# Early first weights, an early third x and modulation products beside the last queries in a two-layer diffusion backbone

## The chip, the cores and the metric

The kernel runs on one core of a Trainium2 chip. The metric is the device time of one execution in microseconds (us). The core has five engines that work from queues of their own, in the order of these queues: PE (matrix products and transposes; the load of its stationary operand is shown as PEld), DVE, ACT and POOL (elementwise work), and SP, which only issues DMAs. POOL issues DMAs too. An engine that waits holds up all that stands behind in its queue.

## The reference

The reference is a backbone of two layers over 512 latent tokens x and 256 context tokens ctx, width 1024, all in fp32. Each layer has three sub-layers: a SwiGLU (hidden width 2816), a token mixer, and a second SwiGLU. Each of them is modulated by a vector c and sandwiched between two norms:

```
for l in range(2):
    mod = silu(c) @ w_ada[l] + b_ada[l]        # nine vectors of 1024; ctx has its own from c_ctx
    for each of the three sub-layers:
        u = rmsnorm(x) * g_pre * (1 + scale) + shift
        y = swiglu(u)  or  mixer(u)
        x = x + gate * rmsnorm(y) * g_post     # the SwiGLUs with another factor of 0.5
```

The even mixer (layer 0) projects u to two inputs of a gated linear recurrence (xa, ga) and to q, k, v of a windowed attention with rotary positions and a sink; the results of both go through one output projection. The odd mixer (layer 1) is a dense attention with normed q and k over context and latent tokens. Context tokens run through all of layer 0 and the first SwiGLU of layer 1; behind it they are needed only for keys and values.

## The kernel before

**Tokens and sub-layers.** The tokens are six tiles of 128 (t = 0, 1 context, 2 to 5 latent), in two chunks c of three tiles (384 columns); the last two sub-layers have four latent tiles, two per chunk. The loop in `body` (L1536 on) runs s = 0 to 5: SwiGLU, even mixer, SwiGLU, SwiGLU, odd mixer, SwiGLU.

**Products.** An fp32 operand is split into two fp32r halves by `halves` (L201): ACT copies it, rounded, into hi, DVE subtracts that from the operand into lo. Each product is then three matmuls (`mm3`, L208). Weights come as 128x1024 fp32 tiles into one of three buffers with the tag raw, and `weights` (L184) splits them, 512 columns at a time, into a hi and a lo buffer (tags whi and wlo, four each). `wtiles` with `one` takes tags ohi and olo instead, two each. `strassen` (L771) does gate and up of a SwiGLU with Strassen's scheme, `down` (L648) its second half, `type2` (L893) the projections of a mixer that leave tokens on partitions (q, k, v, and the output), `type1` (L938) those that leave channels there (xa, ga).

**The boundary between two sub-layers** (`boundary`, L503) runs for each tile of tokens when its y is complete in PSUM: a square with its sum on ACT (L513) and a product with the gate on DVE (L514) for either half, the sum, a reciprocal root (DVE L218, the power on POOL L220), a load of the tile's x by POOL's queue (L522) into one of two buffers with the tag bx, x + gate times normed y on DVE (L524), the store of x by POOL's queue (L528), and the next sub-layer's norm, ACT L426 and POOL L430. `make_u` (L388) then transposes on PE (L435), modulates on ACT and DVE (L409) and splits; where Strassen follows, `Sums` makes differences of blocks on DVE and POOL (L459 to L462). The tiles of chunk 0 are run later, as parts between products that still go on (`later`, `parts`); those of chunk 1 (here b_3, b_4, b_5 by their t) run at once, at the end of the sub-layer, when the products that remain are those of the next.

**Modulation vectors** are made beside other work. `ada_steps` (L113) is a generator for one group p of two 1024-wide vectors: eight steps k, each with two loads of 512 KB by SP's queue into raw tiles wa and four products of 32 columns (recorded as eight matmuls) into one PSUM bank. `tick` (L101) runs the next step of those that are queued in `bg`; groups 3 to 6 are queued at the even mixer (s = 1), 7 and 8 at the odd one (s = 4). `attention` ticks three times per group of heads (L1253), `ffn` once per block. For p > 2 the tiles wa lie in whi and wlo; while a group is under way its bank is held.

**Queries.** In the even mixer `qkv` (called per token tile as its sums are complete) applies the rotary position, splits q into halves qp and transposes them on PE (L1139) into a bank of the two with the tag ps, from which ACT copies (L1140). In the odd mixer `qf` does the same with oqT (L1437).

**What sets the order.** The program order isn't the order in the queues. A planner schedules the program with costs of its own and writes each engine's queue from that; a buffer of a tag is handed on in program order, so a tile waits for the buffer's last reader. `late` and `chain` pin single instructions. Any change of tag or of place in the program can so move work in all queues.

The change touches `weights`, `boundary`, `ada_steps`, `down`, `type1`, `type2`, the two query functions and the loop in `body`.

Of the kernel before, what the change touches and what calls it, by code (L numbers as in the profile page):

```python
# [17 lines left out]
P = 128  # L18
D = 1024
# [9 lines left out]
class Net:  # L29
# [32 lines left out]
    def consts(self):  # L62
        nc, cp, a = self.nc, self.cp, self.a
        self.ident = cp.tile([P, P], F32, name="ident")
        nc.gpsimd.dma_start(self.ident, a["ident"])
        self.sc = cp.tile([P, KD, 32], F32, name="sc")
        nc.sync.dma_start(self.sc, a["cvec"])
        nc.scalar.activation(self.sc, self.sc, AF.Silu)
        self.mhalf = cp.tile([P, 8], F32, name="mhalf")
        nc.vector.memset(self.mhalf, -0.5)  # L70
        self.gpre = cp.tile([P, 6, KD], F32, name="gpre")
        nc.gpsimd.dma_start(self.gpre, a["gpre"])
        self.identr = cp.tile([P, P], F32R, name="identr")
        nc.vector.tensor_copy(self.identr, self.ident)
        self.modc, self.gscale, self.growd = {}, {}, {}
        self.adatile = self.ps

    def c3(self, shape, dt, name):
# [34 lines left out]
    def ada_steps(self, p):  # L113
        nc, cp = self.nc, self.cp
        acc = self.adatile(f"ada{p}")
        for k in range(KD):
            raws = []
            for b in range(2):
                l, j = divmod(2 * p + b, 9)
                src, name = self.a["w_ada"][l, k * P:(k + 1) * P, j * D:(j + 1) * D], f"wa{p}_{k}{b}"  # L120
                if p > 2:

                    t = self.ws.tile([P, D], F32, tag=("whi", "wlo")[b], bufs=4, name=name)
                else:
                    t = self.ws.tile([P, D], F32, tag="bx", bufs=2, name=name)
                nc.sync.dma_start(t, src)
                raws += [t[:, 0:512], t[:, 512:]]
            for g in range(4):
                ins = nc.tensor.matmul(acc[32 * g:32 * g + 32, :], lhsT=self.sc[:, k, :],  # L129
                                       rhs=raws[g], start=(k == 0), stop=(k == KD - 1), skip_group_check=True)  # L130
                if p == 1:
                    self.late(ins)
            yield
# [47 lines left out]
        self.nc.sync.dma_start(t, src)  # L181
        return t

    def weights(self, src, name):  # L184

        raw, n = self.raw(src, name), src.shape[-1]
        hl = [[t[:, i:min(i + 512, n)] for t in ts] for ts in [self.wtiles(n, name)] for i in range(0, n, 512)]
        for i, (hi, lo) in enumerate(hl):
            self.halves(hi, lo, raw[:, i * 512:min(i * 512 + 512, n)])
        return hl  # L190

    def wtiles(self, n, name, one=False):

# [306 lines left out]
                ks = slice(2 * q, 2 * q + 2)  # L500
                self.net.halves(self.u[1][0][:, ks], self.u[1][1][:, ks], self.t4[q], late=True)

    def boundary(self, t, g, xsrc, xdst, nxt, name):  # L503


        nc, bp = self.nc, self.bp
# [1 line left out]
        y1 = bp.tile([P, D], F32, tag="by", bufs=3, name=name + "y")  # L508
        cut = [slice(0, 512), slice(512, D)]
        ss = bp.tile([P, 2], F32, tag="ss", bufs=6, name=name + "s")  # L510

        def half(i, y):
            nc.scalar.activation(self.junk(f"{name}{i}")[:, cut[i]], y, AF.Square, accum_out=ss[:, i:i + 1])  # L513
# [2 lines left out]
        def end():  # L516
# [1 line left out]
            r = self.rms_r(ss[:, 0:1], D, name + "p")  # L518

            def rest():  # L520
                x = bp.tile([P, D], F32, tag="bx", bufs=2, name=name + "x")
                nc.gpsimd.dma_start(x, xsrc(t))  # L522
                for c in cut if nxt is None else [slice(0, D)]:
                    nc.vector.scalar_tensor_tensor(x[:, c], y1[:, c], r[:, 0:1], x[:, c], op0=ALU.mult, op1=ALU.add)  # L524
                    if nxt is None:
                        nc.sync.dma_start(xdst(t)[:, c], x[:, c])
                if nxt is not None:
                    nc.gpsimd.dma_start(xdst(t), x)  # L528
                    self.normed(x, y1, name + "u")
# [118 lines left out]
    def down(self, l, s, n, hd, wt, g, start, finish, hook):  # L648
# [48 lines left out]
        def run():  # L697
# [4 lines left out]
            for k, (i, p) in enumerate(steps):  # L702

                a = min(k + self.AHEAD, len(steps) - 1, (i + 1) * np_ + 1 if p > np_ - 4 else len(steps))
                while todo and steps[a] not in ready:
                    make()
                if (i, p) in parts:
                    j, f = parts[i, p]
                    self.later[j][f]()
# [183 lines left out]
    def type2(self, nm, nk, lhs, nt, wsrc, finish, n=D, hook=None):  # L893
# [9 lines left out]
        for k in range(nk):  # L903
# [7 lines left out]
            if k < nk - self.STAG:  # L911
                for j in range(nt):
                    self.t2mm(accs[j], e, j, nk, n)
            else:
                last.append(e)
        for j in range(nt):

            for half in [0, 512] if nt == 4 and j == 3 else [None]:
# [19 lines left out]
    def type1(self, nm, src, nf, u, finish):  # L938

        for f0 in range(0, nf, 3):  # L940
            fs = range(f0, min(f0 + 3, nf))
            w = [self.weights(src(f), f"{nm}w{f}") for f in fs]
            self.rest()
            acc = [self.acc(f"{nm}a{f}") for f in fs]
            for c in range(2):
# [35 lines left out]
    def even(self, u, gate_i, finish):  # L981
# [132 lines left out]
        def qkv(t, acc):  # L1114
# [18 lines left out]
            nc.vector.tensor_sub(vt[:, :, 1, :], v3, vt[:, :, 0, :].bitcast(F32))  # L1133
            vs[t] = vt
            qt = qst["q"][:, t % 3]
            for h in range(2):
                tp = self.ps(f"qT{t}{h}").bitcast(F32R)
                for e in range(4):
# [231 lines left out]
    def odd(self, u, gate_i, finish):  # L1370
# [49 lines left out]
        def qf(t, acc):  # L1420
# [8 lines left out]
            for s in range(2):  # L1429
                i = 2 * (t - 2) + s  # L1430
                if i % 3 == 0:
                    qtt.append(sb.tile([P, 3, 8, P], F32R, tag=("u0h", "u0l", "u1h")[i // 3], name=f"oqt{i}"))
                qt.append(qtt[i // 3][:, i % 3])
            for h in range(2):
                tp = self.ps(f"oqT{t}{h}")
                for e in range(4):
# [100 lines left out]
    def body(self):  # L1537
# [9 lines left out]
        for s in range(6):  # L1547
            l, sub = divmod(s, 3)
            self.bg += [self.ada_steps(p) for p in need[s]]
            gate = (9 * l + 3 * sub + 2, s < 4)  # L1550
            if s == 5 or s == self.stop:
                un, sn = None, None
                dst = (lambda t: self.out[t * P:(t + 1) * P, :]) if self.stop < 5 else (lambda t: self.out[(t - 2) * P:(t - 1) * P, :])
# [7 lines left out]
            def start(c, j, g, s=s, un=un, sn=sn, xsrc=xsrc, dst=dst):  # L1561
                t = tl[s][c][j]
                nxt = None
                if un is not None:
                    c2, j2 = next((c2, m.index(t)) for c2, m in enumerate(tl[s + 1]) if t in m) if s != 3 else divmod(t, 3)
                    nxt = (9 * ((s + 1) // 3) + 3 * ((s + 1) % 3), un, c2, j2, sn)
                return self.boundary(t, g, xsrc, dst, nxt, f"b{s}_{t}")

            def finish(c, j, end, s=s, un=un, sn=sn):
                if c == 1 and un is not None and len(un) < 2:  # L1570
# [101 lines left out]
```

## Time and profile before

| what | us |
|---|---|
| median of three runs | 2600.66 |
| the three runs | 2595.28, 2600.66, 2603.51 |
| the profiled execution | 2593.1 |
| its span in the profile | 2591.3 |

The profile is of one execution. Times in it are us from the start of the span. The names b_3 to b_5 are the boundary tiles of t = 3 to 5, with the sub-layer's number left out; five boundaries (after s = 0 to 4) begin near 555, 904, 1438, 1948 and 2214 us. The last queries of the even mixer lie at 722 to 737 us, its attention at 737 to 840; those of the odd one at 2050 to 2075 and 2075 to 2165. In names of weights, w0110 is layer 0, second SwiGLU (the digit 1), block 1, gate (0; 1 is up); xaw0 is the first weight of xa, okv0w0 that of the odd mixer's keys and values, eo0w and oo0w those of the output projections.

### The profile page before, as it was taken

How to read it: one execution, taken by the hardware profiler on the slowest of the kernel's cores; microseconds unless marked ns; L12 is line 12 of the kernel's file. 1: busy time of each engine (PE TensorE's matmuls, PEld its weight loads, DVE VectorE, ACT ScalarE, POOL GpSimd, SP SyncE). 2: the span in 40 equal slices, each digit the busy share in tenths (PEclk: the TensorE clock that was granted, in tenths of full speed). 3: DMA queues.
4: the chain of work that ended last, by engine and by line, in shares of the span. 5: the costliest groups of instructions: out<-in, count | busy, mean ns of one | idle time of the engine just before them, and what ended most of it. 6: DMA issues, size and time to landing. Idle time of an engine off the chain costs nothing.

```text
span 2591.3 us, 36846 instructions
## 1 busy us (share of the span) xinstructions
PE 2489.6 (96%) x13683; PEld 2188.9 (84%) x13683; DVE 1877.6 (72%) x2946; ACT 1290.7 (50%) x2346; POOL 373.3 (14%) x472
## 2 busy tenths in 40 slices
PE   7999999998999989999999899999998899999998
PEld 5999997878855779999887899998876667899986
DVE  5877777577677687878757787887586666888843
ACT  4433335556665564443456544444465556655532
POOL 4000000122022130000002300001122221300000
PEclk8999999999999999999999999999999999999999
DMA  7677767651387435555776355558764652544552
GB/s 279 215 244 242 242 222 268 227 188 51 111 297 266 166 106 184 199 180 193 270 245 228 136 187 181 194 193 280 238 233 145 209 180 74 191 130 136 158 174 92
DMA packets 187588, 502.37 MB, mean 194 GB/s; under 512 B 17944, under 2 KB 51912, under 8 KB 187408
## 3 DMA queue, kind: packets, MB, share of 16 engines
q1 hardware_dynamic: 157520, 392.27, 44.6%
q0 software_dynamic: 29888, 107.74, 11.7%
q8 instruction: 107, 1.75, 0.3%
q14 instruction: 73, 0.60, 0.1%
HBM read 397.33 MB, written 102.61 MB: 193 GB/s over the span
## 4 chain that ended last, share of the span: by engine, by line
PE 78%; DVE 7%; issue 7%; DMA 3%; ACT 3%; POOL 2%; SPq 0%; POOLq 0%; DVEq 0%; ACTq 0%
PE px L784 18%; PE py L784 12%; PE pz L784 12%; PE dy L729 8%; PE dx L729 5%; PE d11a L935 5%; PE ada L129 3%; PE oq1a L935 1%; PE gu L211 1%; PE gu L212 1%; PE eo0a L935 1%; PE gu L210 1%; PE qkv1a L935 1%; DMA dw<-in_w_down_dram 1%; PE pT L1332 1%
## 5 line engine op out<-in xcount | busy, mean ns | idle before, releaser
L831 ACT ACTIVATE cp<-px 128x384 f32<-128x384 f32 (+1 forms) x160 | 73.2, 457 | 207.3 <-PE px L784 207.2
L837 ACT ACTIVATE h<-cp 128x768 f32<-128x768 f32 (+1 forms) x80 | 63.3, 792 | 195.7 <-DVE cp L861 138.8
L623 POOL DMA_DIRECT2D wt<-wt x33 | 17.7, 537 | 706.6 <-DVE wt L622 681.4
L129 PE MATMUL ada<-wa,sc 128*32 128x512 f32 x512 | 83.4, 610 | 0.5 <-DVE cols L144 0.4
L831 ACT ACTIVATE cp<-pz 128x384 f32<-128x384 f32 (+1 forms) x80 | 37.0, 463 | 87.2 <-PE pz L784 87.0
L861 DVE TENSOR_TENSOR cp<-px,cp 128x768 f32<-128x768 f32 (+1 forms) x80 | 70.8, 884 | 5.1 <-PE px L784 5.0
L839 DVE TENSOR_TENSOR h<-cp,h 128x768 f32<-128x768 f32 (+1 forms) x80 | 71.2, 891 | 2.2
L670 DVE TENSOR_TENSOR dh_2l<-dh,dh_2h 128x768 fp32r<-128x768 f32 x21 | 20.0, 953 | 70.3 <-ACT dh_2h L669 60.8
L220 POOL TENSOR_TENSOR b_2pr<-b_2pv,mhalf 128x1 f32<-128x1 f32 x6 | 9.6, 1602 | 355.7 <-DVE b_2pv L218 355.7
L811 DVE TENSOR_TENSOR w<-w,w 128x512 f32<-128x512 f32 x80 | 55.4, 692 | 2.7
L812 DVE TENSOR_TENSOR w<-w,w 128x512 f32<-128x512 f32 x80 | 55.4, 692 | 2.7
L810 DVE TENSOR_TENSOR w<-w 128x512 f32<-128x512 f32 x80 | 55.2, 691 | 2.4
L809 DVE TENSOR_TENSOR w<-w,w 128x512 f32<-128x512 f32 x80 | 54.6, 682 | 0.0
L613 POOL DMA_DIRECT2D wt<-in_w_down_dram x66 | 35.5, 537 | 113.1 <-DMA wt<-wt 113.1
L1324 POOL TENSOR_SCALAR p<-p,sm 128x256 f32<-128x256 f32 (+2 forms) x48 | 31.9, 677 | 136.3 <-DVE sm L1321 63.1
L846 DVE TENSOR_TENSOR cp<-py,cp 128x384 f32<-128x384 f32 (+1 forms) x80 | 41.4, 518 | 4.8 <-ACT cp L831 3.9
L670 DVE TENSOR_TENSOR dw_0slo<-dw,dw_0shi 128x1024 fp32r<-128x1024 f32 x21 | 25.7, 1225 | 25.6 <-ACT dw_0shi L669 25.3
L831 ACT ACTIVATE cp<-py 128x384 f32<-128x384 f32 (+1 forms) x80 | 36.3, 454 | 14.3 <-PE py L784 13.9
L1223 ACT ACTIVATE optb<-opT 128x512 fp32r<-128x512 f32 x48 | 28.6, 597 | 28.3 <-PE opT L1520 27.9
L1511 POOL TENSOR_SCALAR op<-op,osm 128x768 f32<-128x768 f32 x32 | 30.6, 956 | 75.8 <-DVE osm L1510 53.4
L854 DVE TENSOR_TENSOR cp<-pz,cp 128x384 f32<-128x384 f32 (+1 forms) x80 | 41.4, 518 | 0.0
L1223 ACT ACTIVATE ptb<-pT 128x512 fp32r<-128x512 f32 x44 | 26.3, 597 | 30.3 <-PE pT L1332 29.9
(5878 smaller groups left out, 9634.2 us busy)
## 6 DMA issues: line engine op xcount, KB each, us to landing
w<-in_wgu_dram SPq DMA_DIRECT2D x175, 512.0 KB, 3.5
wa<-in_w_ada_dram SPq DMA_DIRECT2D x138, 512.0 KB, 5.8
dh<-hd SPq DMA_DIRECT2D x105, 384.0 KB, 5.8
wt<-in_w_down_dram POOLq DMA_DIRECT2D x66, 512.0 KB, 4.6
wt<-wt POOLq DMA_DIRECT2D x66, 512.0 KB, 3.4
dw<-wt SPq DMA_DIRECT2D x60, 512.0 KB, 5.4
hd<-h SPq DMA_DIRECT2D x66, 384.0 KB, 2.8
dw<-in_w_down_dram SPq DMA_DIRECT2D x45, 512.0 KB, 7.0
```

What stands on the lines that cost most here:

```text
L129: ins = nc.tensor.matmul(acc[32 * g:32 * g + 32, :], lhsT=self.sc[:, k, :], rhs=raws[g], start=(k == 0), stop=(k == KD - 1), skip_group_ch ...
L729: nc.tensor.matmul(out, lhsT=x[xi][:, js], rhs=w[wi], start=first and p == 0 and xi == wi, stop=p == np_ - 1 and xi == 1, skip_group_check ...
L784: mm = lambda x, y, **kw: nc.tensor.matmul(out, lhsT=x, rhs=y, skip_group_check=True, **kw)
L810: chain(nc.vector.tensor_add(x1, x1, x2))
L811: chain(nc.vector.tensor_add(x2, x3, x2))
L812: chain(nc.vector.tensor_sub(x4, x4, x2))
L831: chain(nc.scalar.activation(t, src, AF.Copy))
L837: chain(nc.scalar.activation(hc, cp[f], AF.Silu))
L839: chain(nc.vector.tensor_mul(hc, cp[f], hc))
L861: chain(nc.vector.tensor_add(cp[1], x.unsqueeze(1).to_broadcast([P, 2, n]), cp[1]))
L935: mm(acc[:, h:min(h + 512, n)], lhsT=x[xi][:, js], rhs=w[h // 512][wi], start=(k == 0 and xi == 0 and wi == 0), stop=(k == nk - 1 and xi = ...
L1223: self.nc.scalar.activation(b[:, n, 0], tp, AF.Copy)
```

## The change

`ahead` is new. It loads the first weight tile of the next sub-layer (`coming`: xaw0, w0100, w1000, okv0w0, w1100 for s = 0 to 4) into raw and splits it into 512-wide tiles of the tags ohi and olo; `weights` later takes what lies in `pre` instead of loading. It's called in `down` at step (6, 8) of its products and in `type2` of the output projections before their last steps. `boundary` has a new argument: for the tiles of chunk 1 the load of x stands at the boundary's start, and that of t = 5 goes to the tag G1 (one buffer) instead of bx. In `ada_steps` groups 3 and 7 take raw tiles (even k) or G0 and G1 (odd k) rather than whi and wlo, and `qkv` and `qf` tick three steps at t = 4 and five at t = 5, ahead of the transposes. `type1` splits its weights of 1024 columns in one operation per engine rather than two.

```diff
--- before.py
+++ after.py
@@ -73,6 +73,7 @@
         self.identr = cp.tile([P, P], F32R, name="identr")
         nc.vector.tensor_copy(self.identr, self.ident)
         self.modc, self.gscale, self.growd = {}, {}, {}
+        self.pre, self.coming = {}, None
         self.adatile = self.ps
 
     def c3(self, shape, dt, name):
@@ -118,8 +119,11 @@
             for b in range(2):
                 l, j = divmod(2 * p + b, 9)
                 src, name = self.a["w_ada"][l, k * P:(k + 1) * P, j * D:(j + 1) * D], f"wa{p}_{k}{b}"
-                if p > 2:
-
+                if p in (3, 7):
+
+                    tag, bufs = (("raw", 3), (f"G{b}", 1))[k % 2]
+                    t = self.ws.tile([P, D], F32, tag=tag, bufs=bufs, name=name)
+                elif p > 2:
                     t = self.ws.tile([P, D], F32, tag=("whi", "wlo")[b], bufs=4, name=name)
                 else:
                     t = self.ws.tile([P, D], F32, tag="bx", bufs=2, name=name)
@@ -181,13 +185,32 @@
         self.nc.sync.dma_start(t, src)
         return t
 
-    def weights(self, src, name):
-
+    def weights(self, src, name, one=False):
+
+        if name in self.pre:
+            return self.pre.pop(name)
         raw, n = self.raw(src, name), src.shape[-1]
+        if one:
+
+            hi, lo = self.wtiles(n, name)
+            self.halves(hi, lo, raw)
+            return [(hi[:, i:min(i + 512, n)], lo[:, i:min(i + 512, n)]) for i in range(0, n, 512)]
         hl = [[t[:, i:min(i + 512, n)] for t in ts] for ts in [self.wtiles(n, name)] for i in range(0, n, 512)]
         for i, (hi, lo) in enumerate(hl):
             self.halves(hi, lo, raw[:, i * 512:min(i * 512 + 512, n)])
         return hl
+
+    def ahead(self):
+
+        if not self.coming:
+            return
+        name, src = self.coming
+        n = src.shape[-1]
+        raw, hl = self.raw(src, name), []
+        for i in range(0, n, 512):
+            hl.append(self.wtiles(512, f"{name}p{i}", True))
+            self.halves(*hl[-1], raw[:, i:i + 512])
+        self.pre[name] = hl
 
     def wtiles(self, n, name, one=False):
 
@@ -500,7 +523,7 @@
                 ks = slice(2 * q, 2 * q + 2)
                 self.net.halves(self.u[1][0][:, ks], self.u[1][1][:, ks], self.t4[q], late=True)
 
-    def boundary(self, t, g, xsrc, xdst, nxt, name):
+    def boundary(self, t, g, xsrc, xdst, nxt, name, early):
 
 
         nc, bp = self.nc, self.bp
@@ -509,6 +532,15 @@
         cut = [slice(0, 512), slice(512, D)]
         ss = bp.tile([P, 2], F32, tag="ss", bufs=6, name=name + "s")
 
+        def load():
+
+            tag, bufs = ("G1", 1) if t == 5 else ("bx", 2)
+            x = bp.tile([P, D], F32, tag=tag, bufs=bufs, name=name + "x")
+            nc.gpsimd.dma_start(x, xsrc(t))
+            return x
+
+        xs = [load()] if early else []
+
         def half(i, y):
             nc.scalar.activation(self.junk(f"{name}{i}")[:, cut[i]], y, AF.Square, accum_out=ss[:, i:i + 1])
             nc.vector.tensor_mul(y1[:, cut[i]], y, g[:, cut[i]])
@@ -518,8 +550,7 @@
             r = self.rms_r(ss[:, 0:1], D, name + "p")
 
             def rest():
-                x = bp.tile([P, D], F32, tag="bx", bufs=2, name=name + "x")
-                nc.gpsimd.dma_start(x, xsrc(t))
+                x = xs[0] if xs else load()
                 for c in cut if nxt is None else [slice(0, D)]:
                     nc.vector.scalar_tensor_tensor(x[:, c], y1[:, c], r[:, 0:1], x[:, c], op0=ALU.mult, op1=ALU.add)
                     if nxt is None:
@@ -704,6 +735,8 @@
                 a = min(k + self.AHEAD, len(steps) - 1, (i + 1) * np_ + 1 if p > np_ - 4 else len(steps))
                 while todo and steps[a] not in ready:
                     make()
+                if (i, p) == (6, 8):
+                    self.ahead()
                 if (i, p) in parts:
                     j, f = parts[i, p]
                     self.later[j][f]()
@@ -913,6 +946,8 @@
                     self.t2mm(accs[j], e, j, nk, n)
             else:
                 last.append(e)
+        if nm in ("eo1", "oo1"):
+            self.ahead()
         for j in range(nt):
 
             for half in [0, 512] if nt == 4 and j == 3 else [None]:
@@ -939,7 +974,7 @@
 
         for f0 in range(0, nf, 3):
             fs = range(f0, min(f0 + 3, nf))
-            w = [self.weights(src(f), f"{nm}w{f}") for f in fs]
+            w = [self.weights(src(f), f"{nm}w{f}", True) for f in fs]
             self.rest()
             acc = [self.acc(f"{nm}a{f}") for f in fs]
             for c in range(2):
@@ -1133,6 +1168,9 @@
             nc.vector.tensor_sub(vt[:, :, 1, :], v3, vt[:, :, 0, :].bitcast(F32))
             vs[t] = vt
             qt = qst["q"][:, t % 3]
+            if t > 3:
+
+                self.tick(3 if t == 4 else 5)
             for h in range(2):
                 tp = self.ps(f"qT{t}{h}").bitcast(F32R)
                 for e in range(4):
@@ -1431,6 +1469,9 @@
                 if i % 3 == 0:
                     qtt.append(sb.tile([P, 3, 8, P], F32R, tag=("u0h", "u0l", "u1h")[i // 3], name=f"oqt{i}"))
                 qt.append(qtt[i // 3][:, i % 3])
+            if t > 3:
+
+                self.tick(3 if t == 4 else 5)
             for h in range(2):
                 tp = self.ps(f"oqT{t}{h}")
                 for e in range(4):
@@ -1548,6 +1589,8 @@
             l, sub = divmod(s, 3)
             self.bg += [self.ada_steps(p) for p in need[s]]
             gate = (9 * l + 3 * sub + 2, s < 4)
+            self.coming = [("xaw0", a["wi1"][0]), ("w0100", a["wgu"][0, 1, 0, 0]), ("w1000", a["wgu"][1, 0, 0, 0]),
+                           ("okv0w0", a["odd_w_in"][0:P, D:D + 512]), ("w1100", a["wgu"][1, 1, 0, 0]), None][s]
             if s == 5 or s == self.stop:
                 un, sn = None, None
                 dst = (lambda t: self.out[t * P:(t + 1) * P, :]) if self.stop < 5 else (lambda t: self.out[(t - 2) * P:(t - 1) * P, :])
@@ -1564,7 +1607,7 @@
                 if un is not None:
                     c2, j2 = next((c2, m.index(t)) for c2, m in enumerate(tl[s + 1]) if t in m) if s != 3 else divmod(t, 3)
                     nxt = (9 * ((s + 1) // 3) + 3 * ((s + 1) % 3), un, c2, j2, sn)
-                return self.boundary(t, g, xsrc, dst, nxt, f"b{s}_{t}")
+                return self.boundary(t, g, xsrc, dst, nxt, f"b{s}_{t}", c == 1 and un is not None)
 
             def finish(c, j, end, s=s, un=un, sn=sn):
                 if c == 1 and un is not None and len(un) < 2:
```

## Rows read from the trace of the kernel before

**Rows 1.** Busy us, share of the span and instructions per engine (page).

```profile
PE 2489.6 (96%) x13683; PEld 2188.9 (84%) x13683; DVE 1877.6 (72%) x2946; ACT 1290.7 (50%) x2346; POOL 373.3 (14%) x472
```

**Rows 2.** Windows, five boundaries: width, busy PE PEld DVE ACT POOL, PEclk, DMA, GB/s.

```profile
555.00:582.00 27.00, 21.48 (x117) 19.72 (x116) 16.94 (x37) 14.72 (x33) 10.99 (x22) 0.94 0.36 127
904.00:957.00 53.00, 44.45 (x224) 38.81 (x222) 40.72 (x78) 31.52 (x73) 25.14 (x23) 0.94 0.35 121
1438.00:1474.00 36.00, 28.89 (x158) 27.06 (x157) 28.56 (x57) 20.57 (x50) 23.11 (x21) 0.95 0.37 128
1948.00:1972.00 24.00, 20.17 (x91) 15.74 (x91) 19.57 (x39) 16.72 (x36) 10.96 (x13) 0.93 0.49 160
2214.00:2250.00 36.00, 30.02 (x188) 26.43 (x187) 29.37 (x61) 24.64 (x59) 16.61 (x17) 0.95 0.62 205
```

**Rows 3.** Windows at the mixers' last queries and attentions, same columns.

```profile
722.00:737.00 15.00, 9.49 (x60) 6.71 (x58) 8.48 (x31) 11.09 (x40) 4.27 (x8) 0.77 0.81 305
2050.00:2075.00 25.00, 16.25 (x77) 12.62 (x76) 17.09 (x29) 16.12 (x53) 13.78 (x13) 0.86 0.80 289
2050.00:2060.00 10.00, 4.74 (x26) 3.61 (x24) 7.72 (x13) 7.50 (x26) 5.62 (x5) 1.00 0.97 349
737.00:840.00 103.00, 102.17 (x653) 57.93 (x650) 73.93 (x205) 61.03 (x154) 27.78 (x41) 1.00 0.84 294
2075.00:2165.00 90.00, 90.00 (x527) 63.38 (x527) 60.63 (x127) 52.88 (x104) 24.49 (x26) 1.00 0.47 153
```

**Rows 4.** Waits of PE by what ended them: us in all, times, longest.

```profile
PE b_5utp L435 <- POOL b_5y L430: 5.9, 3, 2.5
PE ga0a L210 <- ACT ga0w0hi L203: 5.7, 1, 5.7
PE qT L1139 <- DVE qp L1120: 5.5, 1, 5.5
PE b_4utp L435 <- POOL b_4y L430: 5.4, 4, 2.2
PE oqT L1437 <- DVE osm L1510: 5.1, 1, 5.1
...
PE gu L212 <- DVE w0110lo L203: 4.3, 1, 4.3
```

**Rows 5.** Timeline, first weights: start, us, engine, line, operation, count, [idle <-releaser].

```profile
554.70 0.68 DVE L203 TENSOR_TENSOR xaw0lo<-xaw,xaw0hi 128x512 fp32r<-128x512 f32 x1
...
926.67 0.68 DVE L203 TENSOR_TENSOR w0100lo<-w,w0100hi 128x512 fp32r<-128x512 f32 x1
...
946.70 0.44 PE L212 MATMUL gu<-u_0h,w0110lo 128*128 128x384 f32 x1 [4.26 <-DVE w0110lo L203]
...
1941.08 0.63 ACT L203 ACTIVATE okv0w0hi<-okv0w 128x512 fp32r<-128x512 f32 x1 [1.25 <-DMA okv0w<-in_odd_w_in_dram]
...
2225.45 1.16 ACT L203 ACTIVATE w1100hi<-w 128x512 fp32r<-128x512 f32 x2 [1.55 <-PE oo1a L935]
```

**Rows 6.** Timeline, DVE's addition of the third x at the second boundary.

```profile
943.30 2.28 DVE L524 SCALAR_TENSOR_TENSOR b_5x<-b_5y,b_5pr,b_5x 128x1024 f32<-128x1024 f32 x1 [0.45 <-POOL b_5pr L220]
```

**Rows 7.** Timeline, SP's first load of eo0w, the query transposes, one modulation step.

```profile
709.38 0.33 SPq L181 DMA_DIRECT2D eo0w<-in_even_w_out_dram  x1
...
730.57 0.72 PE L1139 MATMUL qT<-identr,qp 128*128 128x128 f32 x4 [5.50 <-DVE qp L1120]
...
738.13 1.07 PE L129 MATMUL ada<-wa,sc 128*32 128x512 f32 x8
```

**Rows 8.** Timeline, a split of 1024 columns in one on ACT and DVE.

```profile
1425.68 1.04 ACT L669 ACTIVATE dw_6shi<-dw 128x1024 fp32r<-128x1024 f32 x1
...
1427.50 1.22 DVE L670 TENSOR_TENSOR dw_6slo<-dw,dw_6shi 128x1024 fp32r<-128x1024 f32 x1
```

**Rows 9.** Timeline, POOL's sums at the second boundary.

```profile
929.46 4.00 POOL L460 TENSOR_TENSOR b_3y<-b_3uut 128x512 f32<-128x512 f32 x1 [1.00 <-DVE b_3uut L409]
...
939.09 1.28 POOL L460 TENSOR_TENSOR b_4y<-b_4uut 128x512 f32<-128x512 f32 x1 [1.60 <-DVE b_4uut L409]
```

## The prediction

> **What bounds the kernel now.** I began with the busy shares: PE has work for 2489.6 of the span's 2591.3 us [rows 1]. So the change can win only what PE waits, and what a reduced clock costs after such waits. Next I asked where PE is not busy. Windows laid over the five boundaries [rows 2] show, as width less busy PE, 27.00−21.48 = 5.52, 8.55, 7.11, 3.83 and 5.98 us: 31.0 together. Their PEclk of 0.93 to 0.95 says that parts of them run at 1.2 rather than 2.4 GHz, after a gap; width times the missing share is 1.6+3.2+1.8+1.7+1.8 = 10.1 us. The two mixers' last queries lose 5.51+8.75 = 14.3, with 15×0.23+25×0.14 = 7.0 of clock [rows 3]. All that the change can touch is therefore some 62 us of 2600. The waits of PE [rows 4] say what ended these gaps: one first weight (4.3 for w0110lo), the boundary's own chain with its last step on POOL (5.9 and 5.4, before the transposes of the tiles named b_5u and b_4u at several boundaries), and at the queries qp and osm on DVE (5.5 and 5.1).
>
> **The change, part by part.**
> *First weights ahead.* At boundary 1 half of w0100's split stands on DVE at 926.67, 0.68 us in the middle of the boundary's chain [rows 5]; the first product of w0110 waits 4.26 us, to 946.70, for a split that comes behind those of w0100 and w0101 [rows 5]. With w0100 split before the boundary the later tiles move up a place: w0110 is split where w0101 was, and w0111 takes the place that ends about 946.7. It is wanted when w0110's 24 products are done, which could start at 946.70−4.26 = 942.44; at the boundary's mean of 44.45/224 = 0.20 us [rows 2] they take 4.8, to 947.2. So the stall should go; I keep 0.5 of it, as the place may slip by one subtraction: −3.8. At boundary 4 the split of w1100 (ACT 1.16 us for both halves [rows 5]) stands in front of the work of two tiles: about −1.5, all of ACT's and a quarter of DVE's (bounds 0, were it covered, and −2.5, with two DVE halves of 0.68 as well). At boundaries 0 and 2 only half a tile is still unsplit when the boundary starts (xaw0lo, 0.68 us [rows 5]; one row stands for both): −0.7 each. At boundary 3 okv0w0 is split at 1941.08 [rows 5], before the window begins: 0. What the edit adds is the same split inside the product loop before, where PE binds and DVE is busy 72% [rows 1]; if that cover were gone it would be two halves of 0.68 at each of five places, 6.8 us. Sum −3.8−1.5−1.4 = −6.7, bounds +6.8 and −8.2 (4.3, 2.5 and 1.4).
>
> *Third x in its own room.* In the trace the x of tile 5 never ends the wait of its own product: the addition at 943.30 waited its last 0.45 us for the pow of b_5pr on POOL [rows 6]; that row stands for three of the five boundaries, and at the other two the addition did not wait at all. Moving its DMA gives 0, and the 0.60 us of its issue only leave a queue in which nothing was late. Bounds: 0 and −5.9, if the planner, free of the buffer, draws the whole third chain forward and the wait of b_5utp [rows 4] goes.
>
> *Modulation products beside the queries.* Each step of ada is some 1.07 us of PE for its matmuls [rows 7]. Three steps are put before the last tile's sums: 3.2 us that stand on the path. Five more, 5.4 us, fit the gaps of 5.5 and 5.1 before the transposes [rows 4]: 0. Eight steps, 8.6 us, leave each attention. In the odd one PE is busy for all 90.00 us against 60.63 of DVE [rows 3], so all 8.6 count. In the even one PE has 102.17 and DVE 73.93 [rows 3]; of 32 steps (34.2 us) over 11 groups, a group without steps has (102.17−34.2)/11 = 6.2 us of PE and 73.93/11 = 6.7 of DVE, so that the last three groups become DVE's, and give back 3×0.5 = 1.5. One PSUM bank of two is taken until the first attention group, and two halves of the transposes wait out an ACT copy of some 0.6 us (a 128x512 one is 0.63 [rows 5]): +1.2 at each. Even −8.6+3.2+1.5+1.2 = −2.7; odd −8.6+3.2+1.2 = −4.2. With the gaps filled, part of the clock comes back: of 7.0 us I take 2.0, since 14.3−5.5−5.1 = 3.7 us of other waits stay there. In all −8.9. The price that the trace doesn't show is whether the weights are there. Sixteen loads of 0.5 MB (8.4 MB) at the highest rate that I found, 349 GB/s [rows 3], take 24 us. If they start where the raw buffers come free (709.38, where the first of eo0w is issued [rows 7]), the last lands at 733, 2.8 after the transposes at 730.57 [rows 7] and so after the gap: bounds +8.0 (2.8 late at the even mixer and as much at the odd, and a third of the clock's 7.0, 2.4, more) and −17.2−7.0 = −24 (two times 8.6 and all clock).
>
> The Trainium skill, in "Perfetto Trace Analysis", section Roofline, says that one active core is bounded by its 16 DMA engines at about 435 GB/s. By that the 8.4 MB take 19.3 us (an estimate from that page), and the last step would be there before the transposes; the trace's top of 349 is below it, and I kept to the trace.
>
> *Splitting 1024 columns in one.* ga0a waits 5.7 us for its first split on ACT [rows 4]. A half takes 0.63 on ACT and 0.68 on DVE [rows 5], a whole tile of 1024 takes 1.04 on ACT and 1.22 on DVE [rows 8]: PE's first product now waits for the whole, +0.4 on ACT and +0.5 on DVE: +0.8 (bounds 0.4 and 0.9). All other tiles come while PE is busy: 0.
>
> *The clock.* Boundary 1 loses 53×0.06 = 3.2 us by its PEclk [rows 2], after stalls of which two are over 2 us, b_4utp's 2.2 and w0110lo's 4.3 [rows 4]. With the second goes half: −1.6 (0 to −10.1).
>
> Sum: −6.7+0−8.9+0.8−1.6 = −16.4. The profiled execution took 2593.1 us, 1.8 outside its span and 7.6 below the median of 2600.66; I add the change to the median: **2584.3**.
>
> **Rivals.** *The other chain binds (chance 0.24).* POOL's sum of b_3y took 4.00 us where the same form at b_4y took 1.28 [rows 9]. If the wait for b_4y and b_5y on POOL (5.4+5.9) takes the place of the weight's, the weights are worth what leaves before it, 0.7+1.5, and if DVE holds the even attention as well, the modulation products are worth half of the odd mixer's 4.2 alone: −2.2−2.1+0.8 = −3.5, 2597. For it: POOL is the releaser in two of the six waits; against it: w0110lo's is a stall of its own.
> By the Trainium skill's "SBUF — State Buffer", section "Who interferes with whom", a DVE instruction with two SBUF inputs and a GpSimd one that reads SBUF exclude each other for the whole instruction; 4.00 against 1.28 agrees. It speaks against the change: a subtraction moved up still holds POOL, b_4utp's wait of 2.2 stays, and by the rule the result would be this rival's.
>
> *The planner draws the third tile forward (0.13).* Order follows buffers: with x ready the chain of tile 5 moves up and the 5.9 go, the rest of the clock with them (8.5 at boundaries, 10.1 less 1.6; 5.0 at the mixers, 7.0 less 2.0): −16.4−5.9−8.5−5.0 = −35.8, 2565. For it: b_5utp's wait is the largest sum among PE's [rows 4]; against it: in no boundary did x come last.
>
> *Boundaries in a worse order (0.15), on the other side.* Buffers shared with x (G1, raw, the narrow split tiles) change the planner's order, as every tile's due time does. If all five boundaries lose what boundary 1 loses now, 8.55+3.2 = 11.75, that is 58.7−41.1 = +17.6; with the modulation products and the one split −8.9+0.8 it is +9.5, 2610. It ends above the time before from an average loss of 9.8 us per boundary on, (41.1+8.1)/5, where 8.2 are lost now. For it: the same chain loses 8.55 at one boundary and 3.83 at another [rows 2], so order does that much; against it: the split that makes the worst of them is taken out.
>
> **How the numbers follow.** Forecast 0.48, the others 0.24, 0.13 and 0.15. The likeliest one's own range is 2575 to 2594. At 0.3%, 7.8 us, faster means below 2592.9 and slower above 2608.5. Faster: 0.44 of the forecast, 0.05 of the first rival, all 0.13 of the second: 0.62. Slower: 0.12 of the third and 0.01 of the first: 0.13; between: 0.25. The range takes half of the second rival and half of the third: 2561 to 2608, with the ada bounds (−24 and +8 in place of −8.9) inside it.
>
> **What would show it.** Right: the wait of gu for w0110lo under 1; eight L129 steps between the last two tiles' products, and PE's gap before qT and oqT under 1; attentions some 7 and 8.6 us shorter; ga0a's wait at 6.5; b_5utp's wait still near 5.9. Wrong: b_5utp's or b_4utp's wait grows by what the weights gave back; ada's first steps stand in PE's queue with a DMA as releaser; or the clock stays at its 0.77 and 0.86 at the queries, which takes 2 us off the gain.

## The result and the profile after

The changed kernel takes 2611.94 us (median of five, 2610.88 to 2614.70), the kernel before 2597.16 (median of five; the first three had 2600.66): ratio 1.0054, 95% interval 1.0042 to 1.0066. It is slower by some 14 us; forecast were 2584.3 and the range ended at 2608. The profiled execution took 2610.9 us against 2593.1, 17.8 more.

First PE's busy time, from the page of the changed kernel.

```profile
PE 2514.1 (96%) x13683; PEld 2194.2 (84%) x13683; DVE 1883.9 (72%) x2939; ACT 1289.1 (49%) x2339; POOL 380.7 (15%) x472
```

PE issues the same 13683 instructions as in [rows 1] and is busy 24.5 us longer; its waiting went down, from 101.8 us (span less busy) to 95.0. So the loss is not in PE's waits, where the prediction had looked for everything: some work on PE has become dearer. Next the windows, the five boundaries, the two queries and the two attentions, shifted with the changed kernel's own times (columns as in [rows 2, 3]).

```profile
555.00:582.00 27.00, 21.20 (x122) 19.20 (x120) 18.50 (x37) 15.80 (x34) 12.08 (x21) 1.00 0.33 117
921.00:973.00 52.00, 43.26 (x212) 37.40 (x211) 40.41 (x77) 30.60 (x69) 21.69 (x19) 0.91 0.31 105
1457.00:1492.00 35.00, 29.33 (x154) 27.52 (x153) 28.61 (x53) 20.18 (x48) 23.21 (x20) 0.90 0.25 91
1967.00:1991.00 24.00, 18.66 (x84) 14.58 (x83) 18.28 (x38) 15.41 (x35) 10.13 (x12) 0.93 0.52 178
2229.00:2265.00 36.00, 29.37 (x182) 25.66 (x181) 29.61 (x59) 23.97 (x56) 15.97 (x17) 0.95 0.62 203
713.00:734.00 21.00, 19.04 (x119) 9.36 (x118) 11.20 (x36) 12.31 (x45) 4.12 (x8) 1.00 0.72 253
2068.00:2093.00 25.00, 21.43 (x109) 11.80 (x104) 12.87 (x22) 12.88 (x47) 12.35 (x11) 0.93 0.83 292
734.00:854.00 120.00, 117.45 (x625) 61.40 (x625) 76.24 (x202) 61.15 (x153) 24.92 (x37) 1.00 0.64 241
2093.00:2180.00 87.00, 86.52 (x505) 66.08 (x504) 64.46 (x138) 56.22 (x110) 26.78 (x29) 1.00 0.42 153
```

The queries' gaps are filled as forecast, 2.0 us of idle PE instead of 5.5 in the even mixer (with 1.00 for the clock, 0.77 before) and 3.6 instead of 8.8 in the odd one [rows 3]. The boundaries idle 5.8+8.7+5.7+5.3+6.6 = 32.2 us against 31.0 [rows 2], and their clock costs 11.7 us against 10.1: nothing won. But the even attention runs on for 14 us more. Read from the starts of PE's matmuls in each trace (us; e1 and e5 are experiments below):

| from the first matmul of ... to that of ... | before | after | e1 | e5 |
|---|---|---|---|---|
| ga0a, qkv0a (xa and ga) | 52.1 | 46.0 | 45.8 | 47.5 |
| qkv0a, pT (q, k, v of the even mixer) | 70.6 | 77.3 | 75.9 | 71.2 |
| pT, eo0a (even attention) | 120.6 | 135.0 | 114.0 | 114.9 |
| eo0a to px (output projection, boundary 1) | 120.5 | 121.9 | 121.2 | 120.7 |
| oq1a, opT (odd queries) | 51.5 | 59.6 | 59.2 | 52.7 |
| opT, oo0a (odd attention) | 115.9 | 102.7 | 98.5 | 109.1 |

The page's row of the modulation products says what became dearer: busy us and the mean of one, for the kernel before and for the changed one.

```profile
L129 PE MATMUL ada<-wa,sc 128*32 128x512 f32 x512 | 83.4, 610 | 0.5 <-DVE cols L144 0.4
```

```profile
L133 PE MATMUL ada<-wa,sc 128*32 128x512 f32 x512 | 101.0, 607 | 0.9 <-DMA wa<-in_w_ada_dram 0.7
```

The same 512 matmuls, each as long as before, cover 17.6 us more, most of the 24.5. Busy time counts overlapping matmuls once, so fewer of them now run at the same time. PE's timeline in the changed kernel's even attention (start, us, engine, line, operation, count):

```profile
742.67 0.27 PE L1370 MATMUL pT<-ident,p 128*128 128x128 f32 x1
742.87 1.05 PE L133 MATMUL ada<-wa,sc 128*32 128x512 f32 x4
743.86 0.33 PE L1370 MATMUL pT<-ident,p 128*128 128x128 f32 x1
743.94 0.48 PE L1336 MATMUL s<-kth,qt 128*128 128x512 f32 x1
744.26 0.39 PE L1337 MATMUL s<-ktl,qt 128*128 128x512 f32 x1
744.49 0.22 PE L1339 MATMUL s<-maskr,identr 128*128 128x128 f32 x1
744.55 0.60 PE L1370 MATMUL pT<-ident,p 128*128 128x128 f32 x4
745.08 1.05 PE L133 MATMUL ada<-wa,sc 128*32 128x512 f32 x4
```

Before, a step stood as eight records in 1.07 us [rows 7]. Now its two halves, one for each weight tile, stand apart, and each takes 1.05 us: a half costs as much as the whole. The kernel before has steps that stand as one product (two records) and three (six), and these cost the same:

```profile
745.16 1.04 PE L129 MATMUL ada<-wa,sc 128*32 128x512 f32 x2
...
746.79 1.06 PE L129 MATMUL ada<-wa,sc 128*32 128x512 f32 x6
```

The four products of a step write four different sets of 32 partitions and overlap when they are neighbours in PE's queue; one, two or three of them alone take as long as four. Counted in PE's queue, 57 half steps stand apart in the changed kernel, 6 halves and 11 pairs of one and three products in the kernel before.

The Trainium skill, "TensorE: Matmul & The Clock Gate", section "Part 3: Packing small matmuls — row/col tiling", says that small matmuls on different tiles of the array run concurrently. The trace agrees, 1.07 us for four products against 1.05 for two; the prediction had not drawn on it.

### The profile page after: what moved, and what is told of

The parts are those of the page before. It is cut to its first block, busy times and chain, and to the rows that moved or that the text cites. A ratio compares the mean times of both kernels' runs of the same rounds, so it can differ in the third digit from the quotient of the medians.

```text
span 2609.1 us, 36822 instructions
## 1 busy us (share of the span) xinstructions
PE 2514.1 (96%) x13683; PEld 2194.2 (84%) x13683; DVE 1883.9 (72%) x2939; ACT 1289.1 (49%) x2339; POOL 380.7 (15%) x472
## 3 DMA queue, kind: packets, MB, share of 16 engines
q0 software_dynamic: 29888, 107.74, 11.6%
## 4 chain that ended last, share of the span: by engine, by line
PE 78%; issue 7%; DVE 6%; DMA 3%; ACT 3%; POOL 2%; SPq 0%; POOLq 0%; DVEq 0%; ACTq 0%
PE px L817 17%; PE py L817 12%; PE pz L817 12%; PE dy L762 8%; PE dx L762 6%; PE d11a L970 5%; PE ada L133 3%; PE gu L234 1%; PE gu L235 1%; PE gu L233 1%; PE eo0a L970 1%; PE qkv1a L970 1%; DMA dw<-in_w_down_dram 1%; PE qkv0a L970 1%; PE opT L1561 1%
## 5 line engine op out<-in xcount | busy, mean ns | idle before, releaser
L133 PE MATMUL ada<-wa,sc 128*32 128x512 f32 x512 | 101.0, 607 | 0.9 <-DMA wa<-in_w_ada_dram 0.7
L872 DVE TENSOR_TENSOR h<-cp,h 128x768 f32<-128x768 f32 (+1 forms) x80 | 71.3, 891 | 2.2
L701 DVE TENSOR_TENSOR dh_2l<-dh,dh_2h 128x768 fp32r<-128x768 f32 x21 | 20.0, 952 | 71.3 <-ACT dh_2h L700 52.1
L1348 DVE TENSOR_REDUCE mx<-s 128x1 f32<-128x512 f32 (+2 forms) x40 | 27.5, 687 | 25.0 <-PE s L1339 22.2
L1549 ACT ACTIVATE op<-os,onm,orq 128x768 f32<-128x768 f32 x32 | 31.8, 993 | 17.5 <-DVE onm L1547 14.0
```

Source lines behind the costliest of these rows:

```text
L872: chain(nc.vector.tensor_mul(hc, cp[f], hc))
```

## The experiments

The experiments ran in three groups of four (e1 to e4, e5 to e8, e9 to e12), each group on one chip beside the kernel before, whose median lay between 2597.16 (beside the changed kernel) and 2599.16. So a difference between two groups is good to some 2 us, and the ratios correct for it. "Whole steps" ties a step's four products so that they stay neighbours. The last column is the busy time of the modulation products' row shown above, from each profile.

| run | what | us | ratio to before, 95% | ada busy |
|---|---|---|---|---|
| before | | 2597.2 to 2599.2 | 1 | 83.4 |
| after | the change | 2611.94 | 1.0054 (1.0042 to 1.0066) | 101.0 |
| e1_whole | after, whole steps | 2590.83 | 0.9970 (0.9960 to 0.9980) | 68.7 |
| e2_halves | before, halves apart | 2629.99 | 1.0131 (1.0118 to 1.0144) | 114.8 |
| e3_noada | after without the modulation part | 2600.44 | 1.0010 (1.0001 to 1.0019) | 83.3 |
| e4_before_whole | before, whole steps | 2589.84 | 0.9972 (0.9961 to 0.9983) | 72.2 |
| e5_one | e4 and the one split | 2583.01 | 0.9941 (0.9929 to 0.9952) | 71.3 |
| e6_ahead | e4 and first weights ahead | 2598.35 | 1.0003 (0.9994 to 1.0012) | 72.1 |
| e7_early | e4 and early third x | 2593.66 | 0.9980 (0.9971 to 0.9988) | 72.1 |
| e8_ada_one | e5 and the modulation part | 2590.49 | 0.9969 (0.9957 to 0.9981) | 69.0 |
| e9_odd | e5 and its odd half | 2586.85 | 0.9955 (0.9943 to 0.9968) | 71.0 |
| e10_even | e5 and its even half | 2586.76 | 0.9960 (0.9945 to 0.9974) | 69.0 |
| e11_oldtags | after, groups 3 and 7 in the old buffers | 2625.64 | 1.0105 (1.0089 to 1.0120) | 114.9 |
| e12_noticks | after without the early ticks | 2601.38 | 1.0012 (1.0003 to 1.0021) | 86.4 |

**Whole steps and halves: e1, e2, e4.** The tie, in `ada_steps` (e1 on the changed kernel, e4 on the one before):

```diff
-            for g in range(4):
+            held = {}
+            for g in (range(4) if p < 3 else (3, 2, 1, 0)):
                 ins = nc.tensor.matmul(acc[32 * g:32 * g + 32, :], lhsT=self.sc[:, k, :], ...
+                if p > 2:
+                    self.chain(held, ins)
```

e2 does the reverse on the kernel before: a `yield` after g = 1 for p > 2, and in `attention` the step's first half ahead of the transposes (`turn`), its second half at the old place.

```diff
+                if p > 2 and g == 1:
+                    yield
 ...
+                if e in (0,2,3):
+                    self.tick()
                 if e < len(cur.keys):
                     due.append((cur, e, cur.turn(e)))
```

> The changed kernel, but the four matmuls of a modulation step (groups 3 and up) are tied in one order, the second weight tile's first, so that none is ready before all are. Theory: in the changed kernel the two halves of a step stand apart in PE's queue and each half takes as long as a whole step (1.05 us against 1.07), because the four lie in different column groups and run at the same time only when they are neighbours; 57 halves stand apart there, 6 before. Then this takes away some 16 us (even attention from 138 back to some 122 us): about 2595. Rival, the attention is slow because of its order or because DVE binds it without the modulation products as filler: within 3 us of the changed kernel, about 2611.

> The kernel before with one edit: a modulation step is done as two half steps with an attention transposition between them, so that some 29 more pairs of halves stand apart. Theory of halves: each such pair costs another 1.05 us of PE, +25 to +30 us, about 2625, and two matmuls show 1.05 us in the trace. Rival (order or DVE): at most +3 us, about 2600, as PE does the same matmuls.

> The kernel before with the four matmuls of a modulation step tied together as in e1. Theory of halves: only 3 pairs stand apart before, so -3 us at most, about 2595; a larger change would mean that the tie itself does something, and e1 would have to be read with that taken off.

e1 is 21.1 us below the changed kernel and faster than the kernel before. In its trace a step is one group again; the step and the row of the page:

```profile
742.94 1.07 PE L134 MATMUL ada<-wa,sc 128*32 128x512 f32 x8 [0.50 <-DMA wa<-in_w_ada_dram]
```

```profile
L134 PE MATMUL ada<-wa,sc 128*32 128x512 f32 x512 | 68.7, 605 | 2.4 <-DMA wa<-in_w_ada_dram 1.9
```

The row falls by 32.3 us, the time only by 21.1. PE waits 5.8 us more in e1's trace (100.8 against 95.0); where the remainder went wasn't traced.

e2, with no other edit than the order, is 32.5 us above the kernel before. In its trace a half takes what a step does:

```profile
741.97 1.06 PE L129 MATMUL ada<-wa,sc 128*32 128x512 f32 x8
...
743.69 1.05 PE L129 MATMUL ada<-wa,sc 128*32 128x512 f32 x4
...
745.72 1.05 PE L129 MATMUL ada<-wa,sc 128*32 128x512 f32 x4
```

The rival (order of the attention, or DVE) is out: it allowed 3 us at most in both. e4 gained 7.7 us where at most 3 were expected. I had counted only halves, three steps; eight more stand as one and three products in the kernel before and are whole in e4. Eleven times 1.05 is 11.6 us, and the row falls by 11.2, from 83.4 to 72.2. So the kernel before paid part of this price already, and e1 and e4 come out alike (0.9970 and 0.9972): with whole steps on both sides the change is worth nothing. From e4 to e2 the row grows by 42.6 us and the time by 40.1.

**Buffers or ticks: e3, e11, e12.** e3 takes the modulation part out of the changed kernel (tags and ticks), e12 only the two ticks, e11 only the tags:

```diff
-                if p in (3, 7):
-
-                    tag, bufs = (("raw", 3), (f"G{b}", 1))[k % 2]
-                    t = self.ws.tile([P, D], F32, tag=tag, bufs=bufs, name=name)
-                elif p > 2:
+                if p > 2:
```

```diff
-            if t > 3:
-
-                self.tick(3 if t == 4 else 5)
```

> The changed kernel without its part on the modulation products (neither other buffers nor ticks beside the queries); first weights, third x and the one split stay. Both theories: the even attention is back at 122 us, the queries' gaps at 5.5 and 5.1. By the segments of the two traces the part cost 5.1+16.3 in the even mixer and 5.1-9.9 in the odd one, 16.6 in all: about 2595. If the boundaries have lost what the segments there show (+5), it stays 2 to 5 above what the one split (-5.6) gives: 2593 to 2597. By my prediction (first weights -6.7, clock -1.6, one split +0.8) it would be 2590.

> The changed kernel with its ticks beside the queries, but groups 3 and 7 in the old buffers (whi and wlo). In PE's queue 88 half steps stand apart, against 57 in the changed kernel and 6 (with 22 quarters) before. Theory of halves: 15 more pairs at 0.8 to 1.05 us each, about 2626. Rival, the new buffers (raw, G0, G1) are what slows the attention: faster than the changed kernel, 2600.

> The changed kernel with the new buffers of groups 3 and 7 but no ticks beside the queries. 12 half steps stand apart. Theory of halves, which come from the early ticks and not from the buffers: as e3 plus 3 pairs, 2600 to 2605. Rival, the buffers split the steps: as the changed kernel, 2610 or above.

The early ticks set the halves apart, not the buffers: e12 is at 2601.4, e3 at 2600.4 (2593 to 2597 was expected of e3). With the old buffers and the ticks it gets worse, 2625.6 where 2626 was expected; its row says 114.9, 13.9 above the changed kernel, and its time is 13.7 above. Why the planner parts the halves when ticks come early wasn't tried further. e3 also shows that the rest of the change, without the modulation part, is a small loss of 0.1%, not the gain of 7.5 that the prediction's other terms add up to.

**The other parts, one at a time: e5, e6, e7.** Each on e4: e5 with the argument `True` in `type1`'s call of `weights`, e6 with the two calls of `ahead`, e7 with `early` and the tag G1 in `boundary`, each as in the change's diff.

> The kernel before with whole steps (e4) and the one split of 1024 columns in type1; nothing else of the change. In the traces the second half of ga0w0 was split on ACT 16 us after the first, behind other work, and the wait of 5.7 us for it is gone where the split is one operation. Theory: that is the one split's own doing, -5 to -6 against e4, ratio 0.995, about 2584. My prediction's reading (+0.8): 2591. Rival: the first weight in its own buffers (ahead) did it by freeing a place in whi and wlo; then e5 stays at 2590 and e6 shows the gain.

> The kernel before with whole steps (e4) and the first weights split ahead; nothing else of the change. By my prediction -6.7 and -1.6 of clock against e4: 2581. By the segments of e3 (boundaries and output projection +5 to +9 with first weights and third x together): +3 to +8, 2593 to 2598; a boundary whose other chain takes over: 2590.

> The kernel before with whole steps (e4) and the early x of the third tile in its own room; nothing else of the change. By my prediction 0: 2590, within 3 us. If the order of the boundaries suffers from the buffer G1 or from POOL's queue: +3 or more, 2593 to 2597. If the chain of the third tile is drawn forward: -6, 2584.

The one split gains 6.8 us by the medians and 8 by the ratios (0.9941 against 0.9972). In the traces 4.8 of it lie between the first matmul of ga0a and that of qkv0a, 52.3 us in e4 and 47.5 in e5. ACT's timeline in the kernel before shows what [rows 4] didn't say:

```profile
601.51 0.63 ACT L203 ACTIVATE ga0w0hi<-ga0w 128x512 fp32r<-128x512 f32 x1 [5.28 <-PE xaa L211]
...
604.28 3.28 ACT L1036 ACTIVATE lr<-lg,gb 128x768 f32<-128x768 f32 x4
...
611.54 0.84 ACT L203 ACTIVATE xc3h<-xc 128x768 fp32r<-128x768 f32 x1
612.40 1.28 ACT L1051 ACT_TABLE_LOAD   x1
...
617.01 0.92 ACT L1051 ACTIVATE la<-lr,spn 128x768 f32<-128x768 f32 x1
617.84 0.61 ACT L203 ACTIVATE ga0w0hi<-ga0w 128x512 fp32r<-128x512 f32 x1
```

The wait of 5.7 us was for the second half of the tile. The first was split at 601.51, the second 16 us later, behind the recurrence's gates on the same engine. In one operation both are done at the first one's place, as in e5:

```profile
601.90 1.06 ACT L226 ACTIVATE ga0w0hi<-ga0w 128x1024 fp32r<-128x1024 f32 x1 [4.95 <-PE xaa L234]
```

First weights ahead lose 8.5 us (1.0003 against 0.9972). Comparing the starts of the same matmuls in the two traces, e6 falls behind e4 by 3.7 us at the third boundary, 1.5 at the fourth and 4.7 at the fifth, and by little elsewhere. The fourth and the fifth weren't followed further; at the third the trace shows how. POOL and PE in e4:

```profile
1460.32 0.93 POOL L223 TENSOR_TENSOR b_5ur<-b_5uv,mhalf 128x1 f32<-128x1 f32 x1 [0.91 <-DVE b_5uv L221]
1461.35 1.11 POOL L433 TENSOR_SCALAR b_5y<-b_5x,b_5ur 128x1024 f32<-128x1024 f32 x1
...
1462.52 1.09 PE L438 MATMUL b_5utp<-ident,b_5y 128*128 128x128 f32 x8 [1.87 <-POOL b_5y L433]
```

POOL, DVE and PE in e6:

```profile
1457.79 1.60 POOL L483 TENSOR_TENSOR b_4y<-b_4uut 128x512 f32<-128x512 f32 x1 [1.15 <-DVE b_5uv L241]
1459.35 1.02 POOL L243 TENSOR_TENSOR b_5ur<-b_5uv,mhalf 128x1 f32<-128x1 f32 x1
1460.47 2.19 POOL L453 TENSOR_SCALAR b_5y<-b_5x,b_5ur 128x1024 f32<-128x1024 f32 x1
...
1460.46 1.21 DVE L829 TENSOR_TENSOR 1010a1lo<-w,1010a1hi 128x1024 fp32r<-128x1024 f32 x1
...
1462.72 1.54 PE L458 MATMUL b_5utp<-ident,b_5y 128*128 128x128 f32 x6 [4.31 <-POOL b_5y L453]
```

PE has done its weights' products 2.2 us earlier, and transposes at the same time, 1462.7 against 1462.5: the wait grew from 1.87 to 4.31. After it the clock falls to 1.2 GHz: from 1463 to 1467 us e6's granted clock is 0.50, e4's 1.00. The windows of e4 and then of e6, before and behind 1451 us:

```profile
1434.00:1451.00 17.00, 13.40 (x62) 11.47 (x60) 12.49 (x25) 10.29 (x23) 8.25 (x10) 0.90 0.56 186
1451.00:1475.00 24.00, 20.39 (x122) 20.02 (x122) 18.86 (x40) 13.80 (x35) 14.86 (x12) 1.00 0.24 88
```

```profile
1434.00:1451.00 17.00, 13.14 (x68) 11.13 (x66) 12.56 (x25) 10.64 (x23) 8.42 (x10) 1.00 0.57 192
1451.00:1475.00 24.00, 18.41 (x95) 18.10 (x96) 16.64 (x31) 10.33 (x26) 14.40 (x12) 0.86 0.22 77
```

Behind 1451 us e6 loses 24×0.14 = 3.4 us of clock; before, it saves the 17×0.10 = 1.7 that e4 loses there. With PE idle for 9.45 us in both windows against 7.21, the boundary costs some 1.7+2.2 = 3.9 more, which fits the 3.7. DVE's 1010a1lo is a split from behind the boundary; in e6 it stands inside, and POOL's b_5y, 1.11 us in e4 where DVE idles, takes 2.19 beside it. The Trainium skill, "SBUF — State Buffer", section "Who interferes with whom", says that a DVE instruction with two inputs in SBUF contends with a GpSimd (POOL) instruction that reads SBUF, and that the port they share is an exclusive lock; the 2.19 us against 1.11 agree.

The early x is at 0.9980 against 0.9972; the intervals overlap, so 0 was not refuted and a loss of some 2 to 4 us isn't either. The trace of e7 speaks for a loss: it falls 5.1 us behind e4's at boundary 1, where PE's transposes of b_1u wait 3.0 us for ACT instead of 1.4 and the granted clock from 902 to 920 us is 0.91 instead of 1.00. That execution (2597.25) is at the upper end of its group, so the size is open.

**The modulation part with whole steps: e8, e9, e10.** e8 is e1 without `ahead` and early x; e9 has `p in (7,)` and only `qf`'s tick, e10 `p in (3,)` and only `qkv`'s.

> The changed kernel with whole steps, without first weights and without early x: what is left is the modulation products beside the queries and the one split. If the one split gives -5.5 and the modulation products -8.9 by the prediction, 2576; if the first two parts of the change cost nothing, as much as e1, 2591. From e1 less e3's cost of the boundaries I expect 2580 to 2585.

> The kernel before with whole steps, the one split of 1024 columns (together e5) and the modulation products beside the odd mixer's queries alone (group 7). By the segments of e8 against e4 the odd mixer pays 6.8 before its transposes and gets 10.2 back in the attention, -3.4: 2579.6. The forecast's terms say -4.2 and some clock: 2578. Rival: another place of the program loses it again as in e8 (6.5 us in the down product before the odd mixer): 2583 to 2587.

> e5 with the modulation products beside the even mixer's queries alone (group 3), steps whole. The forecast's terms say -2.7 and some clock: 2579. By the segments of e8 the eight steps cost 4.6 ahead of the attention, which gives only 1.9 back, as its last groups wait for their softmax with no modulation product left to fill: +2.7, 2586.

Each is 4 to 8 us slower than e5; of e8 2580 to 2585 was expected, and it took 2590.5. The intervals of e9 and e10 touch that of e5, so their traces have to say it. In e10 the even queries take 3.6 us more (qkv0a to pT, 74.8 against 71.2), the attention 1.5 less (113.4 against 114.9). Windows over the same stretch of attention, for e5 and then e10:

```profile
737.00:842.00 105.00, 100.49 (x675) 60.36 (x675) 80.28 (x213) 68.45 (x168) 27.29 (x41) 1.00 0.82 298
```

```profile
737.00:842.00 105.00, 95.57 (x637) 59.65 (x637) 80.91 (x218) 67.97 (x171) 29.19 (x42) 1.00 0.69 268
```

PE idles 9.4 us instead of 4.5: without modulation products as filler it waits for the softmax and what follows it (in e10's waits s for p on ACT 2.5 us and pT for p on POOL 1.7, neither of them in e5's, and av for ott on DVE 2.6, 2.0 in e5). In e9 the odd mixer pays 8.0 before its transposes and gets 10.7 back, −2.7; but 7.5 us are lost in the down product of the sub-layer before, as in e8 (6.5). DVE and PE there in e9:

```profile
1910.79 1.28 DVE L558 SCALAR_TENSOR_TENSOR b_2x<-b_2y,b_2pr,b_2x 128x1024 f32<-128x1024 f32 x1 [7.37 <-DMA b_2x<-xd]
1911.99 0.95 DVE L704 TENSOR_TENSOR dh_8l<-dh,dh_8h 128x768 fp32r<-128x768 f32 x1
...
1915.09 0.79 PE L763 MATMUL dx<-dw_8slo,dh_8h 128*128 128x512 f32 x1 [4.75 <-DVE dw_8slo L704]
```

An addition that waits for its x stands ahead of a split that PE needs; in e5 the split of dh_8 comes first (1903.04) and the addition at 1910.41 waits for nothing. Why the planner turned them isn't settled. e5 beats both kernels: 2583.01, 14 to 16 us below the kernel before, by whole steps and the one split.

## Why the prediction was wrong

- **"Eight steps, 8.6 us, leave each attention" failed**, with "each step of ada is some 1.07 us of PE". 1.07 is the price of a group of neighbours, and half a group costs the same. What the edit does to the steps that stay in the attentions was put at nothing; it set their halves apart, 57 instead of 6. The tie takes 21.1 us off the changed kernel and 7.7 off the one before, so some 13 of the 14 us of the loss are this, and the sign with it. The rest of the miss is that with whole steps on both sides the change is worth 0 and not −16.4; the next points say why. The rows for the price stood there: eight matmuls in 1.07 us [rows 7], with a mean of 0.61 us each on the page, can only be overlap.
- **The even attention would not have given its 8.6 anyway**: forecast were 1.5 of them given back to DVE; e10 shows 1.5 us gained in all, since steps fill waits of the softmax chain. The odd mixer came near its term, −2.7 against −4.2.
- **The weights' supply** was no problem in that size: ada waited 0.7 us for its DMA in the changed kernel, 1.9 with whole steps (e1).
- **First weights, −6.7: wrong sign**, +8.5 by e6. The step "so the stall should go" held for w0110lo at boundary 1 and failed one step later. PE's waits in the changed kernel, from 921 to 970 us:

```profile
PE b_5utp L458 <- POOL b_5y L453: 2.3, 1, 2.3
PE b_4utp L458 <- POOL b_4y L453: 2.2, 1, 2.2
PE gu L235 <- DVE w0111lo L226: 1.5, 1, 1.5
```

The 4.3 us [rows 4] became 1.5 for the next tile and 2.3 for b_5y: the first rival's mechanism, the chain over POOL in the place of the weight. Over the whole run PE's waits for b_4y and b_5y on POOL grew from 5.4+5.9 = 11.3 us [rows 4] to 14.2:

```profile
PE b_4utp L458 <- POOL b_4y L453: 9.4, 5, 2.9
...
PE b_5utp L458 <- POOL b_5y L453: 4.8, 3, 2.3
```

It explains this term, not the time.
- **Third x, 0**: not refuted by e7's time, though its trace speaks for a loss.
- **One split, +0.8: wrong sign**, −6.8 by e5. A row of PE's waits sums tiles by name; I took "ga0w0hi" for the first half without looking where its two halves stand on ACT.
- **The clock, −1.6: wrong sign** at boundary 1, 52×0.09 = 4.7 us lost against 3.2. Where the waits took the weight's place the clock is no better than before (0.78 from 961 to 971 us, against 0.83 from 944 to 954), and from 921 to 931 us it is 0.83, where the kernel before has 1.00 (904 to 914). At the queries more came back than the 2.0 us of the forecast: 0.77 to 1.00 in the even mixer and 0.86 to 0.93 in the odd one, 15×0.23+25×0.07 = 5.2.
- **The third rival** named the right side and, by chance, the time (2610); its place was wrong, since the boundaries lost only 32.2+11.7−41.1 = 2.8 us.

The parts don't add up exactly. From e4's 2589.84, the one split (−6.8), first weights (+8.5), early x (+3.8) and e8's modulation part (+7.5, of which 6.5 in a place where e1 has none of it) give 2596 without those 6.5; e1 is 2590.8. Some 5 us remain unexplained.

## What to carry to other kernels

Where matmuls share the array, price the group of neighbours and count how often the order keeps them together; a planner may part them, and a tie that starts with the last operand keeps them whole. Before taking filler work out of an in-order queue, look at what the queue waits for without it. A weight that is ready earlier only helps up to the next thing PE waits for. If PE then waits longer in one piece, look at the clock behind it too: behind the 4.31 us in e6 it was 0.50 for 4 us, behind the 1.87 in e4 it stayed at 1.00.

## What the runs showed of the hardware

Two products of 32 columns (four records of 0.6 us) take 1.05 us and four (eight records) 1.06 to 1.07, in the same kernel and at a granted clock of 1.00 (e2, 741 to 747 us); one alone takes 1.04 (the kernel before). Splitting the steps changed the time by nearly the growth of that one row: 42.6 us of row and 40.1 us of time from e4 to e2, 13.9 and 13.7 from the changed kernel to e11. Putting them together in the changed kernel (e1) gave less, 21.1 us of time for 32.3 of row. POOL's 128x1024 product took 1.11 us with DVE idle and 2.19 beside a DVE subtraction with two inputs (e4, e6).
